# Two of four block sums of the feed-forward weights formed by accumulating DMAs, with the signs of two blocks changed

## Chip, cores and metric

The kernel runs on one core of a Trainium2 chip. The metric is the device time of one execution in microseconds. A core has five engines with a queue each: PE (matrix products), DVE and POOL (elementwise), ACT (elementwise with functions), SP (here it only starts DMAs), and 16 DMA engines, which all queues share.

## The reference

One encoder layer in float32: 512 tokens of width 2048, a mixer of two attentions, then a gated feed-forward network of width 5632. The change touches only the two products that lead from the normed tokens h2 to the feed-forward width:

```python
h2 = rms_norm(x, norm2_w[l]) * (1.0 + sc2) + sh2
ff = (jax.nn.silu(h2 @ w_ffn_gate[l]) * (h2 @ w_ffn_up[l])) @ w_ffn_down[l]
x = x + g2 * ff
```

## The kernel before

**Precision.** PE multiplies a reduced float32 type here. Each float32 tile is split into a high part (a copy on ACT, line 118) and a low part (the rest, a subtraction on DVE, line 119), and each product is made of three matmuls: high by high, high by low, low by high (lines 126 to 128).

**Seven products instead of eight.** Gate and up are computed as 2x2 block products by a scheme of Strassen's kind (Winograd's form): seven block products of sums of blocks instead of eight of blocks. A group (`group7`, line 816) makes 512 columns of gate or of up for all 512 tokens. It adds up over four steps of 512 rows of the weight. 11 groups of columns, gate and up, less the first of gate, which is made with eight products while the tokens' sums are still being formed, give 21 groups and 84 steps.

**One step.** `wforms` (line 767) loads a piece of 512 rows and 512 columns with two DMAs of 512 KB: four blocks b11, b12 (upper rows) and b21, b22 (lower rows), each 128 partitions x 512 numbers. DVE forms four sums: t1 = b12 - b11 and t2 = b22 - t1, the two halves of tile `ta`; t3 = b22 - b12 and t4 = t2 - b21, the two halves of `tb`. Then four tiles are split into high and low: b11 (half a tile), b21 with b22, `ta` and `tb`. Which product uses which half stands in `HALVES[0]`, and PE takes the products in the order of `ORDER`: 1, 2, 3, 5, 6, 7, 4. A product is 12 matmuls of 128x128 by 128x256, so a step has 84.

**Tokens' side.** `xforms` (line 788) forms the same kind of sums of the token blocks a11 to a22 on DVE and POOL, once for each of the four steps, ahead of all groups. Its tiles `sa` and `sb` use the buffers of `ta` and `tb`.

**Group ends.** The seven products stand in seven of the eight banks (`BANK`). After the fourth step ACT copies product 1 and DVE forms the four output blocks (lines 833 to 840) from the banks; the next group writes the same banks. After each up group the two results are multiplied (line 911) and stored (line 912, 1 MB).

**Buffers and order.** Loads into `raw` have 5 buffers, `ta` 2, `tb` 1, the split tiles `whi` and `wlo` 5 each, of which a step uses four, so that the split of one step's tile waits for PE to leave the tile five before it. All plain loads are issued from SP in order. A planner in the tile framework sets the order of instructions in each queue from its own estimates, and so may put work of the next step ahead of the rest of this one; waits on semaphores are put in by the framework.

```python
    ORDER = (1, 2, 3, 5, 6, 7, 4)
    HALVES = ((1,), (2, 3), (5, 6), (7, 4)), ((1,), (2, 4), (5, 6), (7, 3))
    BANK = {1: "mm", 2: "mm", 3: "mm", 5: "mm", 6: "S", 7: "S", 4: "Y"}
```

Of the kernel before, what the change touches and what calls it, by code (L numbers as in the profile page):

```python
# [15 lines left out]
ALU = mybir.AluOpType  # L16
AX = mybir.AxisListType

P = 128
# [65 lines left out]
def encoder_block(ctx: ExitStack, tc, xp, c, w_ada, b_ada, norm1_w, w_in, q_norm_w, k_norm_w, tb,  # L85
                  w_oa, w_ob, w_out, norm2_w, w_gate, w_up, w_down, final_w, rope, wmask, out):
    nc = tc.nc
    V, S, G = nc.vector, nc.scalar, nc.gpsimd
# [11 lines left out]
    def wtile(tag, at=None):  # L100
        at = wbufs["at"] if at is None else at
        return wp.tile([P, 1024 + wbufs["pad"]], F32R, tag=tag, name=tag, bufs=wbufs["w"])[:, at:at + 1024]
    dram = ctx.enter_context(tc.tile_pool(name="dram", bufs=1, space=bass.MemoryType.DRAM))

    def bank(tag):
        return ps.tile([P, 512], F32, tag=tag, name=tag, bufs={"mm": 4, "S": 2, "T": 1, "Y": 1}[tag])
# [10 lines left out]
    def split(hi, lo, src, eng=V):  # L117
        S.activation(hi, src, AF.Copy)  # L118
        eng.tensor_sub(lo, src, hi)  # L119

    def pair(pool, tag, width, bufs):
        return (pool.tile([P, width], F32R, tag=tag + "h", name=tag + "h", bufs=bufs),
                pool.tile([P, width], F32R, tag=tag + "l", name=tag + "l", bufs=bufs))

    def mm3(o, lh, ll, rh, rl, start, stop, **kw):
        nc.tensor.matmul(o, lh, rh, start=start, stop=False, **kw)  # L126
        nc.tensor.matmul(o, lh, rl, start=False, stop=False, **kw)  # L127
        nc.tensor.matmul(o, ll, rh, start=False, stop=stop, **kw)  # L128

    def unit(w, k0, nk, c0, ncol):  # L130
        raw = wp.tile([P, 1024], F32, tag="raw", name="raw", bufs=wbufs["raw"])
        r3 = raw[:, :nk * ncol].rearrange("p (k n) -> p k n", k=nk)
        nc.sync.dma_start(r3, w[k0 * P:(k0 + nk) * P, c0:c0 + ncol].rearrange("(k p) n -> p k n", p=P))
        return raw[:, :nk * ncol], r3
# [96 lines left out]
    t1 = const.tile([P, KT], F32, name="t1")  # L231
# [269 lines left out]
    q = pair(p_a, "q", 4 * T, 1)  # L501
# [56 lines left out]
    q = pair(p_a, "q", 4 * T, 1)  # L558
# [119 lines left out]
    for j in range(0, KT, 2):  # L678
        form1([w_ob], j * P, 2, yT_b, [[bank("mm"), bank("mm")]],
              gated(sg_b[j:], lambda e, g, b: merge(j + e, g, b)))  # L680
        if j >= KT - 6 and len(pre) < 2:
            raw = p_pre.tile([P, 1024], F32, name="praw", tag="praw")
            k0 = 2 * len(pre)
            nc.sync.dma_start(raw.rearrange("p (k n) -> p k n", k=2),
                              w_out[k0 * P:(k0 + 2) * P, :512].rearrange("(k p) n -> p k n", p=P))
            hl = pair(p_pre, f"p{k0}", 1024, 1)
# [62 lines left out]
    HALVES = ((1,), (2, 3), (5, 6), (7, 4)), ((1,), (2, 4), (5, 6), (7, 3))  # L749
# [5 lines left out]
    def half(t, n=2):  # L755
        return t.rearrange("p (a q n) -> p a q n", q=2, n=256) if n == 2 else t.rearrange("p (q n) -> p q n", q=2)

    def split7(parts, tiles, kinds):

        d = {}  # L760
        for (src, views), (hi, lo), rs in zip(parts, tiles, kinds):
            split(hi, lo, src)
            for r, v in zip(rs, views):
                d[r] = (v(hi), v(lo))
        return d

    def wforms(w, k0, c0):
        rt = []
        for a in range(2):
            raw, r3 = unit(w, k0 + 2 * a, 2, c0, 512)  # L770
            rt.append((raw, r3[:, :, :256], r3[:, :, 256:]))
        (_, b11, b12), (r1, b21, b22) = rt
        ta = wp.tile([P, 1024], F32, tag="ta", name="ta", bufs=2)
        tb = wp.tile([P, 1024], F32, tag="tb", name="tb", bufs=1)
        t1, t2_ = (half(ta)[:, a] for a in range(2))
        t3, t4 = (half(tb)[:, a] for a in range(2))
        V.tensor_sub(t1, b12, b11)
        V.tensor_sub(t2_, b22, t1)
        V.tensor_sub(t3, b22, b12)
        V.tensor_sub(t4, t2_, b21)  # L780
        hl = [[wtile(t) for t in ("whi", "wlo")] for _ in range(4)]
        col = lambda e: lambda t: t.rearrange("p (q n) -> p q n", q=2)[:, :, e * 256:(e + 1) * 256]
        blk = lambda e: lambda t: half(t)[:, e]
        g0 = [t[:, :512].rearrange("p (q n) -> p q n", q=2) for t in hl[0]]
        return split7(((b11, (lambda t: t,)), (r1, (col(0), col(1))), (ta, (blk(0), blk(1))), (tb, (blk(0), blk(1)))),
                      [g0] + hl[1:], HALVES[0])

    def xforms(pool, e, o, full=False):

        sa = wp.tile([P, 1024], F32, tag="ta", name="sa", bufs=2)  # L790
        sb = wp.tile([P, 1024], F32, tag="tb", name="sb", bufs=1)
        a11, a21 = e[:, :512], e[:, 512:]
        a12, a22 = o[:, :512], o[:, 512:]
        V.tensor_add(sa[:, :512], a21, a22)
        V.tensor_sub(sa[:, 512:], sa[:, :512], a11)
        G.tensor_sub(sb[:, :512], a11, a21)
        G.tensor_sub(sb[:, 512:], a12, sa[:, 512:])
        tl = [[pool.tile([P, 512 if n == 0 else 1024], F32R, tag=f"x{n}{t}", name=f"x{n}{t}") for t in "hl"]
              for n in range(4)]
        blk = lambda n: lambda t: t[:, n * 512:(n + 1) * 512].rearrange("p (q n) -> p q n", q=2)  # L800
        d = {}
        if full:
            h21 = [wtile(t, 0)[:, :512] for t in ("whi", "wlo")]
            split(*tl[0], a11)
            split(*h21, a21)
            split(*tl[1], o)
            d["21"] = tuple(blk(0)(t) for t in h21)
            for n, rs in ((0, (1,)), (1, (2, 4))):
                for j, r in enumerate(rs):
                    d[r] = tuple(blk(j)(t) for t in tl[n])  # L810
            d.update(split7(((sa, (blk(0), blk(1))), (sb, (blk(0), blk(1)))), tl[2:], HALVES[1][2:]))
            return d
        return split7(((a11, (blk(0),)), (o, (blk(0), blk(1))), (sa, (blk(0), blk(1))), (sb, (blk(0), blk(1)))),
                      tl, HALVES[1])

    def group7(wsrc, xs, order, dst):

        bk = {r: bank(BANK[r]) for r in ORDER}
        for n, s in enumerate(order):
            w = wsrc(s)  # L820
            for r in ORDER:
                (wh, wl), (xh, xl) = w[r], xs[s][r]
                for q in range(2):
                    for c in range(2):
                        o = bk[r][:, c * 256:(c + 1) * 256]
                        cs = slice(c * P, (c + 1) * P)
                        first, last = n == 0 and q == 0 and c == 0, n == len(order) - 1 and q == 1
                        mm3(o, wh[:, q, cs], wl[:, q, cs], xh[:, q], xl[:, q], first, last, skip_group_check=True)
        p = {r: b.rearrange("p (c n) -> p c n", c=2) for r, b in bk.items()}
        (d11, d12), (d21, d22) = dst  # L830
        with tc.high_priority():
            p1 = io.tile([P, 512], F32, tag="io", name="p1").rearrange("p (c n) -> p c n", c=2)
            S.activation(p1, p[1], AF.Copy)
            V.tensor_add(d11, p[2], p1)
            V.tensor_add(d21, p[6], p1)
            V.tensor_add(d12, p[5], d21)
            V.tensor_add(d12, p[3], d12)
            V.tensor_add(d21, p[7], d21)
            V.tensor_add(d22, p[5], d21)
            V.tensor_sub(d21, d21, p[4])  # L840


    wbufs["at"] = 16
# [4 lines left out]
    def raw_tile(name):  # L848
        return wp.tile([P, 1024], F32, tag="raw", name=name, bufs=wbufs["raw"])
# [46 lines left out]
    for n in range(FU):  # L896
        cs = []
        for w in (w_gate, w_up):
            c, v = c_tile()
            cs.append(c)  # L900
            if n == 0 and w is w_gate:
                for f in range(4):
                    S.activation(v[:, f // 2, :, f % 2], banks[f].rearrange("p (t n) -> p t n", t=2), AF.Silu)
                continue
            dst = (v[:, 0, 0], v[:, 1, 0]), (v[:, 0, 1], v[:, 1, 1])
            group7(lambda s: wforms(w, 4 * s, n * 512), hx, range(SU), dst)
            if w is w_gate:
                S.activation(c, c, AF.Silu)
        for a in range(2):
            sl = slice(a * 1024, (a + 1) * 1024)  # L910
            V.tensor_mul(cs[1][:, sl], cs[1][:, sl], cs[0][:, sl])
        (nc.sync if n < FU - 1 else nc.scalar).dma_start(ff_d[n], cs[1])
# [66 lines left out]
    for cc in range(4):  # L979
        hi, lo = pair(p_l, f"w{cc}", 4 * 512, 1)  # L980
        for k in range(0, 4, 2):
            raw, _ = unit(w_down, f0 + k, 2, cc * 512, 512)
# [52 lines left out]
```

## Time and profile before

| what | value |
|---|---|
| median of 3 runs | 2708.28 us (2704.64 to 2709.36) |
| profiled execution | 2707.57 us, span 2705.8 us |
| PE busy | 2602.3 us (96%) |
| DVE busy | 1782.6 us (66%) |
| ACT busy | 968.3 us (36%) |
| POOL busy | 132.9 us (5%) |
| mean granted TensorE clock | 0.986 |

The span runs from the first to the last instruction; 1.8 us of the execution lie outside it. A row of a group reads: line, engine, operation, written tile `<-` read tiles, shapes, count, busy us in all, mean ns of one, and the idle time just before with what ended it. A row of waits reads: waiting engine, its tile and line, `<-`, the releasing engine, tile and line, then us in total, times, and the longest. Instructions that only start a DMA do not count as busy, so SP does not show in the table. `SPq` and `POOLq` are the issuing queues.

### The profile page before, as it was taken

What the parts mean: (1) busy time and instruction counts of PE and PEld (TensorE: products, weight loads), DVE (VectorE), ACT (ScalarE), POOL (GpSimd) and SP (SyncE); (2) the same over time, 40 slices, a digit from 0 to 9 for tenths busy, and PEclk for the clock granted to TensorE, in tenths of its full rate; (3) what the DMA queues carried; (4) which work ended last, traced back from release to release, by engine and by line L of the source; (5) the groups of instructions that cost most, each with busy time, mean ns of one, the idle gap of its engine ahead of it and who ended that gap; (6) DMA issues with size and microseconds to landing.
All of it is one profiled execution on the core that took longest, in us unless ns stands there. A gap on an engine that the chain in (4) does not pass through costs nothing.

```text
span 2705.8 us, 38742 instructions
## 1 busy us (share of the span) xinstructions
PE 2602.3 (96%) x15385; PEld 2286.1 (84%) x15385; DVE 1782.6 (66%) x2556; ACT 968.3 (36%) x1323; POOL 132.9 (5%) x90
## 2 busy tenths in 40 slices
PE   6999898999999998999889999999999999999997
PEld 5788686878888887877789999999999988888886
DVE  7994747356656566665668888888888864343227
ACT  6233344123323233322544444444444432132122
POOL 0001331300000000000010000000000000000000
PEclk9999999999999999999989999999999999999999
DMA  9873233565554677496333433333333455243332
GB/s 307 279 248 117 75 114 105 186 189 161 173 165 150 210 257 233 148 327 212 120 112 120 137 129 124 109 128 125 125 126 125 135 190 182 94 155 125 102 109 86
DMA packets 277157, 427.17 MB, mean 158 GB/s; under 512 B 17008, under 2 KB 140256, under 8 KB 274416
## 3 DMA queue, kind: packets, MB, share of 16 engines
q1 hardware_dynamic: 276640, 423.59, 47.9%
q8 instruction: 121, 1.98, 0.3%
q10 hardware_dynamic: 336, 1.11, 0.1%
q14 instruction: 60, 0.49, 0.1%
HBM read 392.11 MB, written 32.52 MB: 157 GB/s over the span
## 4 chain that ended last, share of the span: by engine, by line
PE 70%; DMA 6%; DVE 4%; ACT 1%; issue 1%; SPq 0%; POOL 0%; DVEq 0%; ACTq 0%; POOLq 0%
PE mm L128 15%; PE mm L127 15%; PE mm L126 15%; PE S L127 5%; PE S L126 5%; PE S L128 5%; DMA raw<-in_w_ada 4%; PE Y L126 2%; PE Y L127 2%; PE Y L128 2%; DVE acc L261 1%; PE T L126 1%; PE T L128 1%; PE T L127 1%; DVE wlo L119 1%
## 5 line engine op out<-in xcount | busy, mean ns | idle before, releaser
L118 ACT ACTIVATE whi<-raw 128x1024 fp32r<-128x1024 f32 (+1 forms) x465 | 453.9, 978 | 988.7 <-PE mm L127 282.1
L119 DVE TENSOR_TENSOR wlo<-raw,whi 128x1024 fp32r<-128x1024 f32 (+1 forms) x433 | 483.1, 1118 | 376.2 <-ACT whi L118 375.6
L261 DVE SCALAR_TENSOR_TENSOR acc<-raw,cact,acc 128x512 f32<-128x512 f32 (+1 forms) x368 | 275.9, 757 | 165.7 <-DMA raw<-in_w_ada 160.5
L119 DVE TENSOR_TENSOR wlo<-ta,whi 128x1024 fp32r<-128x1024 f32 x84 | 102.7, 1223 | 71.5 <-ACT whi L118 71.4
L118 ACT ACTIVATE whi<-ta 128x1024 fp32r<-128x1024 f32 x84 | 89.4, 1065 | 132.1 <-PE mm L127 132.1
L118 ACT ACTIVATE whi<-tb 128x1024 fp32r<-128x1024 f32 x84 | 89.6, 1067 | 123.9 <-PE S L127 123.9
L128 PE MATMUL mm<-x1h,wlo 128*128 128x256 f32 x400 | 110.4, 276 | 0.0
L126 PE MATMUL mm<-x1h,whi 128*128 128x256 f32 x400 | 110.4, 276 | 0.0
L127 PE MATMUL mm<-x1l,whi 128*128 128x256 f32 x400 | 110.4, 276 | 0.0
L119 DVE TENSOR_TENSOR wlo<-tb,whi 128x1024 fp32r<-128x1024 f32 x84 | 102.5, 1221 | 6.3 <-ACT whi L118 3.1
L126 PE MATMUL mm<-x0h,whi 128*128 128x256 f32 x368 | 102.7, 280 | 3.3 <-ACT whi L118 3.3
L128 PE MATMUL mm<-x0h,wlo 128*128 128x256 f32 x368 | 103.1, 280 | 0.8 <-DVE wlo L119 0.8
L127 PE MATMUL mm<-x0l,whi 128*128 128x256 f32 x368 | 102.8, 279 | 0.0
L119 POOL TENSOR_TENSOR wlo<-raw,whi 128x1024 fp32r<-128x1024 f32 x32 | 77.7, 2431 | 407.0 <-ACT whi L118 376.0
L128 PE MATMUL Y<-x1h,wlo 128*128 128x256 f32 x336 | 92.7, 276 | 0.0
L126 PE MATMUL mm<-x3h,whi 128*128 128x256 f32 x336 | 92.7, 276 | 0.0
L127 PE MATMUL mm<-x3l,whi 128*128 128x256 f32 x336 | 92.7, 276 | 0.0
L128 PE MATMUL mm<-x3h,wlo 128*128 128x256 f32 x336 | 92.7, 276 | 0.0
L126 PE MATMUL mm<-x2h,whi 128*128 128x256 f32 x336 | 92.7, 276 | 0.0
L127 PE MATMUL mm<-x2l,whi 128*128 128x256 f32 x336 | 92.7, 276 | 0.0
L128 PE MATMUL mm<-x2h,wlo 128*128 128x256 f32 x336 | 92.7, 276 | 0.0
L126 PE MATMUL S<-x2h,whi 128*128 128x256 f32 x336 | 92.7, 276 | 0.0
(1793 smaller groups left out, 7883.6 us busy)
## 6 DMA issues: line engine op xcount, KB each, us to landing
raw<-in_w_in SPq DMA_DIRECT2D x133, 512.0 KB
raw<-in_w_ada SPq DMA_DIRECT2D x256, 256.0 KB
raw<-in_w_gate SPq DMA_DIRECT2D x88, 512.0 KB
raw<-in_w_up SPq DMA_DIRECT2D x88, 512.0 KB
raw<-in_w_down SPq DMA_DIRECT2D x88, 512.0 KB
raw<-in_w_ada SPq DMA_DIRECT2D x64, 512.0 KB
raw<-in_w_out SPq DMA_DIRECT2D x38, 512.0 KB
ffr<-ffd SPq DMA_DIRECT2D x22, 512.0 KB
```

The lines of the kernel that those rows point to most:

```text
L118: S.activation(hi, src, AF.Copy)
L119: eng.tensor_sub(lo, src, hi)
L126: nc.tensor.matmul(o, lh, rh, start=start, stop=False, **kw)
L127: nc.tensor.matmul(o, lh, rl, start=False, stop=False, **kw)
L128: nc.tensor.matmul(o, ll, rh, start=False, stop=stop, **kw)
L261: V.scalar_tensor_tensor(acc, part, cact[:, k:k + 1], acc, op0=ALU.mult, op1=ALU.add)
```

## The change

b11 is now loaded alone by a DMA of 256 KB into a `raw` tile, b21 with b22 by one of 512 KB as before. b11 is loaded a second time into one half of `ta`, and b22 into the other half, each by a DMA of 256 KB from SP. Then two accumulating DMAs of 256 KB issued from POOL add b12, read from DRAM, to both halves. So `ta` now holds t1 = b11 + b12 and t3 = b12 + b22 without work of DVE, and DVE forms t2 = t1 + b22 and t4 = t2 + b21 in `tb`. b12 no longer gets a tile of its own. The order of products stays; the halves of the tiles now belong to products 5 and 7 (`ta`) and 6 and 4 (`tb`).

Only sums are formed this way, so the signs of blocks b12 and b21 in the scheme are turned against before, and to make up for it those of a12 and a22 in the tokens' sums and some in the output sums.

```diff
     def wforms(w, k0, c0):
-        rt = []
-        for a in range(2):
-            raw, r3 = unit(w, k0 + 2 * a, 2, c0, 512)
-            rt.append((raw, r3[:, :, :256], r3[:, :, 256:]))
-        (_, b11, b12), (r1, b21, b22) = rt
+        blk_of = lambda a, e: w[(k0 + 2 * a) * P:(k0 + 2 * a + 2) * P,
+                                c0 + 256 * e:c0 + 256 * (e + 1)].rearrange("(q p) n -> p q n", p=P)
+        b11 = raw_tile("b11")[:, :512]
+        nc.sync.dma_start(half(b11, 1), blk_of(0, 0))
+        r1, r3 = unit(w, k0 + 2, 2, c0, 512)
+        b21, b22 = r3[:, :, :256], r3[:, :, 256:]
         ta = wp.tile([P, 1024], F32, tag="ta", name="ta", bufs=2)
         tb = wp.tile([P, 1024], F32, tag="tb", name="tb", bufs=1)
-        t1, t2_ = (half(ta)[:, a] for a in range(2))
-        t3, t4 = (half(tb)[:, a] for a in range(2))
-        V.tensor_sub(t1, b12, b11)
-        V.tensor_sub(t2_, b22, t1)
-        V.tensor_sub(t3, b22, b12)
-        V.tensor_sub(t4, t2_, b21)
+        t1, t3 = (half(ta)[:, a] for a in range(2))
+        t2_, t4 = (half(tb)[:, a] for a in range(2))
+        for t, a, e in ((t1, 0, 0), (t3, 1, 1)):
+            nc.sync.dma_start(t, blk_of(a, e))
+        for t in (t1, t3):
+            nc.gpsimd.dma_start(t, blk_of(0, 1), accum_op=ALU.add)
+        V.tensor_add(t2_, t1, b22)
+        V.tensor_add(t4, t2_, b21)
...
-        g0 = [t[:, :512].rearrange("p (q n) -> p q n", q=2) for t in hl[0]]
-        return split7(((b11, (lambda t: t,)), (r1, (col(0), col(1))), (ta, (blk(0), blk(1))), (tb, (blk(0), blk(1)))),
-                      [g0] + hl[1:], HALVES[0])
+        g0 = [t[:, :512] for t in hl[0]]
+        return split7(((b11, (lambda t: half(t, 1),)), (r1, (col(0), col(1))), (ta, (blk(0), blk(1))), (tb, (blk(0), blk(1)))),
+                      [g0] + hl[1:], ((1,), (2, 3), (5, 7), (6, 4)))
...
-        V.tensor_add(sa[:, :512], a21, a22)
+        V.tensor_sub(sa[:, :512], a21, a22)
         V.tensor_sub(sa[:, 512:], sa[:, :512], a11)
         G.tensor_sub(sb[:, :512], a11, a21)
-        G.tensor_sub(sb[:, 512:], a12, sa[:, 512:])
+        G.tensor_add(sb[:, 512:], a12, sa[:, 512:])
...
-            V.tensor_add(d12, p[5], d21)
+            V.tensor_sub(d12, p[5], d21)
             V.tensor_add(d12, p[3], d12)
             V.tensor_add(d21, p[7], d21)
-            V.tensor_add(d22, p[5], d21)
-            V.tensor_sub(d21, d21, p[4])
+            V.tensor_sub(d22, p[5], d21)
+            V.tensor_add(d21, p[4], d21)
```

## The prediction

> **What bounds the kernel now.** I read the profile from coarse to fine: busy tenths over the span, busy time inside the feed-forward stage, who waits there, then one step of it in order of time. First the slices, each 67.6 us wide.
>
> ```profile
> PE   6999898999999998999889999999999999999997
> DVE  7994747356656566665668888888888864343227
> PEclk9999999999999999999989999999999999999999
> DMA  9873233565554677496333433333333455243332
> ```
>
> TensorE is full nearly everywhere. The changed function runs where VectorE stands at 8 (slices 22 to 32). Busy time in four stretches there (columns: stretch, its length, busy us of PE, its weight loads, DVE, ACT, POOL, then clock, share of the 16 DMA engines, GB/s):
>
> ```profile
> 1400.00:1600.00 200.00, 200.00 (x1767) 200.00 (x1767) 164.93 (x203) 89.77 (x96) 0.00 (x0) 1.00 0.37 119
> 1600.00:1800.00 200.00, 200.00 (x1768) 200.00 (x1767) 172.56 (x215) 88.00 (x92) 0.00 (x0) 1.00 0.39 127
> 1800.00:2000.00 200.00, 200.00 (x1767) 200.00 (x1766) 170.61 (x210) 86.30 (x91) 0.00 (x0) 1.00 0.39 127
> 2000.00:2190.00 190.00, 190.00 (x1679) 190.00 (x1678) 160.08 (x197) 83.98 (x88) 0.00 (x0) 1.00 0.38 123
> ```
>
> A busy PE alone could hide short gaps, since its records overlap. The view of waits from 1400 to 2190 us settles it: its whole list of waiters holds ACT and DVE only.
>
> ```profile
> ACT whi L118 <- PE mm L127: 186.1, 165, 4.4
> ACT whi L118 <- PE Y L127: 133.8, 81, 1.7
> ACT whi L118 <- PE S L127: 122.2, 72, 1.7
> DVE wlo L119 <- ACT whi L118: 111.2, 106, 4.3
> ACT whi L118 <- PE Y L128: 1.9, 1, 1.9
> DVE ta L778 <- DMA raw<-in_w_up: 1.4, 3, 0.8
> ACT whi L118 <- ACT whi L118: 0.2, 1, 0.2
> ```
>
> PE never waits; ACT waits for PE to give back the split tiles, DVE waits for ACT. So this stage ends when the matmuls end, at 1.00 granted clock, and DVE at 668.2 of 790 us (85%) is not the bound. One step (one call of the weight function and its 84 matmuls) is read off ACT's order:
>
> ```profile
> 1801.55 1.06 ACT L118 ACTIVATE whi<-ta 128x1024 fp32r<-128x1024 f32 x1 [1.60 <-PE mm L127]
> ...
> 1807.04 0.64 ACT L118 ACTIVATE whi<-raw 128x512 fp32r<-128x512 f32 x1 [1.66 <-PE Y L127]
> ...
> 1816.56 0.64 ACT L118 ACTIVATE whi<-raw 128x512 fp32r<-128x512 f32 x1 [1.65 <-PE Y L127]
> ```
>
> A split into the slot that the last product Y leaves starts at 1807.04 and again at 1816.56: a step is 9.52 us, a product 1.36 us (a seventh). 84 steps make 800 us.
>
> **What the change removes.** Lines 777 and 779:
>
> ```profile
> L777 DVE TENSOR_TENSOR ta<-raw x84: 676/691/694, 1389.4 to 2175.9; 128x512 f32<-128x512 f32 x84
> ```
>
> ```profile
> L779 DVE TENSOR_TENSOR tb<-raw x84: 679/691/695, 1391.1 to 2187.5; 128x512 f32<-128x512 f32 x84
> ```
>
> 2 x 84 x 0.691 = 116 us of DVE. They stand under a full PE, so they give 0 us. The two other subtractions become additions of the same shape: 0. The signs in the x forms and in the output sums change operations, not shapes or engines: 0.
>
> **What it adds, on the DMA engines.** A step issued two 512 KB loads from SP; now SP issues one of 512 KB and three of 256 KB, and POOL two accumulating ones of 256 KB. Rows are 1 KB where they were 2 KB. The price of a packet comes from two stretches, this stage (1400 to 2200) and one with mostly 1 KB rows (600 to 900). Columns: packets, MB, share of 16 engines.
>
> ```profile
> q1 hardware_dynamic: 46587, 98.01, 37.7%
> ```
>
> ```profile
> q1 hardware_dynamic: 45523, 49.24, 52.0%
> ```
>
> 0.377 x 16 x 800 us / 46587 = 103.6 ns for about 2 KB; 0.520 x 16 x 300 / 45523 = 54.8 ns for about 1 KB. A step has 9.52 x 16 = 152.3 us of engine time. Plain loads: 256 x 103.6 + 768 x 54.8 ns = 68.6 us. The rest of the stage (98.01 MB less 161 loads of 0.524 = 13.6 MB, 14% of the 37.7%) takes 8.0 us a step. For 512 accumulating packets no row exists. Low end: the plain 54.8 ns. High end, an estimate: four times that, 219 ns. I take 103.6 ns, the row of the 2 KB packet, because an accumulating packet must also read 2 KB (1 KB from DRAM, 1 KB of the tile). Sum 68.6 + 8.0 + 53.0 = 129.6 of 152.3 us: 85%, from 38%. It fits; it would cease to fit at (152.3 - 76.6) / 512 = 148 ns.
>
> The Trainium skill (Collectives: The Full Stack, section "The bandwidth ceiling: the fold count and why AG ≠ RS ≠ AR") says that an adding transfer runs at half the rate because it has to read two sources. By it a packet would be 2 x 54.8 = 109.6 ns and the load 87%, the same verdict; no run here shows it yet.
>
> **What it adds, in time from buffer to buffer.** Now tile ta (two buffers) is loaded, not computed: SP waits until the tile of two steps earlier is split, loads b11 and b22 into the halves, POOL waits for that and adds b12 to both, then DVE and ACT may read. These rows of DVE give the release and the two places where the result is wanted:
>
> ```profile
> 1802.65 1.22 DVE L119 TENSOR_TENSOR wlo<-ta,whi 128x1024 fp32r<-128x1024 f32 x1 [1.44 <-ACT whi L118]
> 1803.90 0.69 DVE L777 TENSOR_TENSOR ta<-raw 128x512 f32<-128x512 f32 x1
> ```
>
> ```profile
> 1816.20 0.69 DVE L779 TENSOR_TENSOR tb<-raw 128x512 f32<-128x512 f32 x1
> 1816.81 0.69 DVE L780 TENSOR_TENSOR tb<-ta,raw 128x512 f32<-128x512 f32 x1
> ```
>
> Released at 1803.87. The sum t2 for that tile would stand about where L779 stands two steps on, at 1816.20: 12.3 us later. The split of the tile itself falls two steps after 1801.55, at 1820.59: 16.7 us later. So up to 12.3 us nobody notices; up to 16.7 us DVE's queue stands behind t2; beyond that every two steps grow by the excess. What the chain takes comes from two loads of 512 KB:
>
> ```profile
> 1808.60 0.37 SPq L133 DMA_DIRECT2D raw<-in_w_gate  x1
> ```
>
> ```profile
> 1810.70 0.37 SPq L133 DMA_DIRECT2D raw<-in_w_gate  x1
> ```
>
> ```profile
> 1809.00:1809.50 0.50, 0.50 (x6) 0.50 (x6) 0.05 (x1) 0.41 (x1) 0.00 (x0) 1.00 0.00 0
> 1809.50:1810.00 0.50, 0.50 (x7) 0.50 (x6) 0.50 (x1) 0.00 (x0) 0.00 (x0) 1.00 0.48 78
> ...
> 1813.00:1814.00 1.00, 1.00 (x11) 1.00 (x10) 0.97 (x2) 0.16 (x1) 0.00 (x0) 1.00 0.65 242
> 1814.00:1815.00 1.00, 1.00 (x11) 1.00 (x11) 0.87 (x3) 0.91 (x1) 0.00 (x0) 1.00 0.01 4
> ```
>
> The engines are idle until past 1809.50, so bytes move some 1.15 us after the issue at 1808.60; the second load is done about 3 us after its issue. A 256 KB load is 1.15 + 256 x 54.8 / 16 ns = 2.0 us, the second 0.9 us more. For POOL's part in an accumulation (it must issue it, perhaps work on it) there is no row. Low end 0; high end one POOL operation over a 128x1024 tile:
>
> ```profile
> L119 POOL TENSOR_TENSOR wlo<-raw,whi 128x1024 fp32r<-128x1024 f32 x32 | 77.7, 2431 | 407.0 <-ACT whi L118 376.0 <-PE mm L128 17.7 <-PE S L128 13.3
> ```
>
> I take the high end, 2.4, to be safe; then 1.15 to the first byte and 256 x 103.6 / 16 ns = 1.7 us: 5.3 us for one. The first half is ready at 2.0 + 5.3 = 7.3 us, the second, if both run strictly one after the other, at 12.6. With POOL at 0, plain packets and both at once it is 4.9. If the next step's b11 and r1 (2.5 us of engines) get between, 15.1. All below 16.7, and the first half below 12.3: 0 us.
>
> **What moves.** The last pair of blocks changes from {5,6} {7,4} to {5,7} {6,4}: tb is wanted one product earlier (1.36 us), and its slot comes free one product later. Split of tb now starts 6 products into the step before (8.2 us), takes about 2.3 us (as ta: 1801.55 to 1803.87) and is needed after 9.52 + 4 x 1.36 = 15.0 us: 4.5 us spare, 0 us. SP issues 4 DMAs a step at 0.37 us, 1.5 of 9.52 us; the stores of c stand in the same queue. POOL ran nothing in this stage. If the cover goes (PE no longer full), all this DMA waiting shows at once.
>
> **Sum:** 0 us against the profiled execution's 2707.57 us (span 2705.8). The median of the runs shown is 2708.28, 0.7 above. I forecast 2707.5, with an own range of 2702 to 2713.
>
> **Rivals, all but the last slower.**
>
> (1) Late at group ends: 2739 us. Seven banks are emptied by DVE between the steps of two groups.
>
> ```profile
> 1864.16 0.64 ACT L118 ACTIVATE whi<-raw 128x512 fp32r<-128x512 f32 x1 [1.65 <-PE Y L127]
> ```
>
> ```profile
> 1867.09 0.68 DVE L839 TENSOR_TENSOR c<-mm,c 128x512 f32<-128x512 f32 x1
> ```
>
> The new group starts at 1864.16 and wants bank 5 three products later, 1868.24; L839 gives it back at 1867.77. Spare: 0.5 us. If t2 waits for both halves (12.6 us) and a 1 MB store of c (2 x 1.66 us of engines) gets between, it comes at 15.9, 3.6 us after its place; DVE's evacuations queue behind it, and PE loses 3.1 us at each of 10 stores: 31 us. Against it: DVE has 1.4 us a step more room. A stall can also cost clock:
>
> ```profile
> 1380.00:1382.00 2.00, 0.49 (x2) 0.49 (x3) 2.00 (x3) 2.00 (x3) 0.88 (x1) 0.80 0.00 0
> 1382.00:1384.00 2.00, 1.59 (x8) 1.29 (x7) 2.00 (x2) 2.00 (x4) 1.26 (x1) 0.50 0.00 0
> ```
>
> (2) The round trip is the bound: 2775 us. Each us beyond 16.7 costs half a us per step, 42 us in all. If POOL took 4 us per accumulation, 15.1 + 2 x 1.6 = 18.3: 1.6 x 42 = 67 us. For it: no row prices POOL's part. It decides from 3.2 us per accumulation on.
>
> The Trainium skill (SBUF — State Buffer, section "Who interferes with whom") warns that DMAs issued from POOL starve while VectorE holds the port pair both share, and advises the other queues. It exempts two-input operations, which all those of this stage are; no trace here shows either.
>
> (3) The DMA engines are full: 2752 us at three times the plain packet: (76.6 + 512 x 0.1644) / 16 = 10.05 us a step, 0.53 x 84 = 44 us; at four times 11.8 us a step, 2899. Decides from 148 ns on. For it: 1 KB rows and a load of 85% before any queueing.
>
> (4) Faster, 2700: another order in the queues at the stage's two ends, where PE does idle. Nothing in the body can give.
>
> **Chances.** Forecast 0.46, (1) 0.17, (2) 0.17, (3) 0.14, (4) 0.06. This kernel's runs spread by 0.17%, so I call 0.2% (5.4 us) no change: same 0.46, slower 0.48, faster 0.06. The range 2702 to 2800 holds the forecast, (1), most of (2) and the lower half of (3).
>
> **What will show it.** Right: no PE line among the stage's waits, steps of 9.52 us, DVE lower by 1.4 us a step, DMA share near 0.85. Rival 1: PE waiting for DVE once per group, DVE waiting for a DMA into ta. Rival 2: ACT or DVE waiting for ta's DMA at every step with engines below full. Rival 3: DMA share at 1. I am wrong if PE has gaps inside a group.

## The result, and the profile after

The changed kernel takes 2824.76 us in the median of four runs (2823.7 to 2827.16), against 2708.82 us of the kernel before beside it: a ratio of 1.0429, 95% interval 1.041 to 1.0447. The profiled execution took 2824.1 us with a span of 2822.3, 116.5 us more than before. The first split of a `ta` starts at 1401.92 us (1401.76 before), and the last multiplication of gate by up at 2327.08 instead of 2210.39 (before, then after). So the whole loss, 116.7 us, arises between the two, in the changed stage. Beside the experiments below, several kernels, the one before among them, have single runs near 2740 us, about 30 us above their others; why was not examined.

```profile
2210.39 2.35 DVE L911 TENSOR_TENSOR c<-c 128x1024 f32<-128x1024 f32 x2
```

```profile
2327.08 2.35 DVE L914 TENSOR_TENSOR c<-c 128x1024 f32<-128x1024 f32 x2
```

The four stretches of that stage again, same columns (length, busy us of PE, weight loads, DVE, ACT, POOL, clock, DMA share, GB/s):

```profile
1400.00:1600.00 200.00, 186.41 (x1582) 185.31 (x1581) 121.42 (x142) 77.34 (x86) 43.77 (x36) 0.97 0.74 178
1600.00:1800.00 200.00, 184.80 (x1535) 183.56 (x1533) 121.36 (x143) 71.29 (x81) 43.83 (x36) 0.94 0.74 177
1800.00:2000.00 200.00, 185.06 (x1544) 183.87 (x1545) 127.41 (x151) 70.97 (x79) 44.04 (x37) 0.97 0.76 184
2000.00:2190.00 190.00, 175.25 (x1469) 173.90 (x1468) 117.21 (x138) 66.80 (x75) 42.40 (x35) 0.96 0.75 182
```

PE now has gaps: 731.5 of 790 us busy, 58.5 us idle. It also runs slower while it is busy: 6130 matmuls at the 113.2 ns of before (790 us / 6981) would be 693.7 us, so 37.8 us more went to slower matmuls. Together 96 of 790 us. The granted clock explains most of the 37.8: its shortfall (0.03, 0.06, 0.03 and 0.04) times the four stretches is an estimated 32 us. The rest stays open, because PE also has slow stretches at full clock. In the following one, 30 us hold 257 matmuls, where 113.2 ns each would give 265:

```profile
1850.00:1880.00 30.00, 30.00 (x257) 30.00 (x257) 17.86 (x21) 12.32 (x14) 7.30 (x6) 1.00 0.77 188
```

DVE is emptier than ever and the DMA engines are at three quarters.

The waits of the whole stage (1400 to 2300 us), longest first:

```profile
POOL ta L781 <- issue: 619.0, 140, 7.9
DVE wlo L119 <- ACT whi L118: 278.5, 87, 5.9
ACT whi L118 <- DMA ta<-in_w_gate: 239.8, 36, 9.0
ACT whi L118 <- DMA ta<-in_w_up: 152.9, 26, 7.7
PEld mm L126 <- issue: 73.0, 26, 5.1
PE mm L126 <- DVE c L840: 64.7, 19, 4.9
```

Read from below: PE waits for DVE's evacuation L840, 19 times, once in nearly every one of the 21 groups (53.3 of the 58.3 us that it waits from 1400 to 2190), and the weight loads (PEld) stand idle for about as long; ACT waits 62 times for the DMAs into `ta`; and POOL, which issues those, stands 140 times in a wait that no semaphore ends ("issue"). All accumulating DMAs of the run, as a line of the program (duration is what POOL spends on one, landing counts from its issue):

```profile
L781 POOL DMA_DIRECT2D ta<-in_w_up x88: 1203/1213/1317, 1383.6 to 2308.5; - x88
L781 POOL DMA_DIRECT2D ta<-in_w_gate x80: 1204/1213/1224, 1431.6 to 2263.4; - x80
...
DMA to landing us min/median/max: 4.2/4.7/8.8
```

168 of them from 1383.6 to 2308.5 us: one every 5.54 us. Two per step make 11.1 us, where PE needs 9.52. POOL's queue in order of time:

```profile
1825.44 1.22 POOL L781 DMA_DIRECT2D ta<-in_w_gate  x1 [3.55 <-issue]
1831.34 1.21 POOL L781 DMA_DIRECT2D ta<-in_w_up  x1 [4.68 <-issue]
1836.12 1.22 POOL L781 DMA_DIRECT2D ta<-in_w_up  x1 [3.57 <-issue]
1841.21 1.21 POOL L781 DMA_DIRECT2D ta<-in_w_up  x1 [3.87 <-issue]
```

Each starts 4.8 to 5.9 us after the one before, about when that one has landed. The program does not ask for this: in the list of POOL's instructions the second accumulation of a tile waits for its own plain load (DMAHW) alone, the first also for DVE and for the accumulations (DMASW) of the tile two back. None waits for the accumulation just before it.

```
101 L781 DMA ta_12598<-in_w_up 128x2x256 [waits DMASW5_49,DMAHW0_49,DMASW4_49,DVE_49]
102 L781 DMA ta_12598<-in_w_up 128x2x256 [waits DMAHW1_49]
103 L781 DMA ta_12710<-in_w_up 128x2x256 [waits DMASW7_49,DMAHW4_49,DMASW6_49,DVE_49]
104 L781 DMA ta_12710<-in_w_up 128x2x256 [waits DMAHW5_49]
```

What a late accumulation does to PE is seen at a group's end. First ACT:

```profile
1840.99 1.06 ACT L118 ACTIVATE whi<-ta 128x1024 fp32r<-128x1024 f32 x1 [5.91 <-DMA ta<-in_w_up]
```

Then DVE:

```profile
1842.09 1.23 DVE L119 TENSOR_TENSOR wlo<-ta,whi 128x1024 fp32r<-128x1024 f32 x1 [3.05 <-ACT whi L118]
1843.23 0.68 DVE L838 TENSOR_TENSOR c<-S,p 128x512 f32<-128x512 f32 x1
1843.95 0.69 DVE L839 TENSOR_TENSOR c<-mm,c 128x512 f32<-128x512 f32 x1
1844.67 0.69 DVE L840 TENSOR_TENSOR c<-mm,c 128x512 f32<-128x512 f32 x1
```

Then PE:

```profile
1845.51 0.55 PE L126 MATMUL mm<-x3h,whi 128*128 128x256 f32 x1 [3.79 <-DVE c L840]
```

ACT's split of `ta` waits for the DMA, DVE's low part waits for ACT, and the evacuations of the group just finished stand behind it in DVE's queue, so PE does not get back the bank that its third product needs (line 840 reads it last). The same moment in stretches of 2 us, with the clock:

```profile
1842.00:1844.00 2.00, 0.00 (x0) 0.00 (x0) 1.88 (x3) 2.00 (x4) 0.43 (x1) 1.00 0.36 48
1844.00:1846.00 2.00, 0.49 (x2) 0.52 (x3) 1.97 (x4) 0.47 (x1) 0.03 (x1) 0.87 1.02 192
1846.00:1848.00 2.00, 2.00 (x12) 2.00 (x10) 2.00 (x3) 0.00 (x0) 1.19 (x1) 0.50 0.51 158
1848.00:1850.00 2.00, 2.00 (x15) 2.00 (x15) 2.00 (x4) 1.07 (x1) 0.00 (x0) 0.78 0.91 128
```

After a gap of 3.8 us PE goes on at half the clock, which is back at 1.00 in the stretch from 1850 us on.

The software queue of the new DMAs, same stretch of 900 us (packets, MB, share of 16 engines):

```profile
q0 software_dynamic: 44316, 42.72, 33.2%
```

0.332 x 16 x 900 us / 44316 = 107.9 ns a packet. An accumulation (0.262 MB) has 272 packets.

### The profile page after: what moved, and what is told of

It is laid out like the page before. It is cut to its first block, busy times and chain, and to the rows that moved or that the text cites. A ratio compares the mean times of both kernels' runs of the same rounds, so it can differ in the third digit from the quotient of the medians.

```text
span 2822.3 us, 39236 instructions
## 1 busy us (share of the span) xinstructions
PE 2648.6 (94%) x15385; PEld 2324.7 (82%) x15385; DVE 1673.2 (59%) x2388; ACT 950.3 (34%) x1323; POOL 336.9 (12%) x258
## 4 chain that ended last, share of the span: by engine, by line
PE 43%; DMA 16%; issue 10%; DVE 10%; ACT 2%; POOL 1%; SPq 0%; DVEq 0%; ACTq 0%; POOLq 0%
PE mm L126 10%; PE mm L128 10%; PE mm L127 10%; DMA ta<-in_w_gate 5%; DMA raw<-in_w_ada 4%; DMA ta<-in_w_up 4%; DVE wlo L119 4%; PE S L127 3%; PE S L126 3%; PE S L128 3%; DVE acc L261 1%; PE Y L126 1%; PE Y L127 1%; ACT whi L118 1%; PE Y L128 1%
## 5 line engine op out<-in xcount | busy, mean ns | idle before, releaser
L118 ACT ACTIVATE whi<-raw 128x1024 fp32r<-128x1024 f32 (+1 forms) x381 | 399.6, 1051 | 816.2 <-PE mm L127 246.3
L119 DVE TENSOR_TENSOR wlo<-raw,whi 128x1024 fp32r<-128x1024 f32 (+1 forms) x349 | 426.0, 1221 | 327.9 <-ACT whi L118 326.9
L126 PE MATMUL mm<-x3h,whi 128*128 128x256 f32 x336 | 102.2, 304 | 64.7 <-DVE c L840 64.7
L781 POOL DMA_DIRECT2D ta<-in_w_up x88 | 107.2, 1218 | 369.1 <-issue 318.4
L781 POOL DMA_DIRECT2D ta<-in_w_gate x80 | 97.4, 1217 | 352.5 <-issue 313.4
L126 PEld LDWEIGHTS mm<-x3h,whi 128*128 128x128 f32 x336 | 69.6, 207 | 67.9 <-issue 67.9
L126 PE MATMUL mm<-x2h,whi 128*128 128x256 f32 x336 | 100.5, 299 | 4.6 <-DVE c L842 3.6
L128 PE MATMUL mm<-x2h,wlo 128*128 128x256 f32 x336 | 99.2, 295 | 2.4 <-DVE wlo L119 2.3
L128 PE MATMUL mm<-x3h,wlo 128*128 128x256 f32 x336 | 100.3, 298 | 0.0
L127 PE MATMUL mm<-x3l,whi 128*128 128x256 f32 x336 | 100.2, 298 | 0.0
```

The source lines that it names most:

```text
L781: nc.gpsimd.dma_start(t, blk_of(0, 1), accum_op=ALU.add)
```

## Experiments

My theory: the accumulating DMAs run one at a time, and their queue is too slow for the step. First rival: the round trip through the two buffers of `ta` is too long. Second: the DMA engines are too full. Times are medians; each ratio is to the kernel before, run beside it on the same chip, with its 95% interval. It is estimated from the single runs and is not the quotient of the medians.

**A third buffer of `ta`** (one of `raw` given up for it).

```diff
-    wbufs.update(raw=5, w=5, pad=64)
+    wbufs.update(raw=4, w=5, pad=64)
-        ta = wp.tile([P, 1024], F32, tag="ta", name="ta", bufs=2)
+        ta = wp.tile([P, 1024], F32, tag="ta", name="ta", bufs=3)
```

> The changed kernel with three buffers of ta (and four of raw to make room). Theory S (the accumulating DMAs of POOL run one at a time, 168 of them at about 5.5 us, 11 us a step where PE needs 9.52): the rate of the queue is not touched, 2800 to 2835 us, whole list of accumulating DMAs still 5.3 to 5.6 us apart on average. Rival L (the round trip through two buffers of ta is too long, 18 us where 16.7 are free): a third buffer gives 9.5 us more, so 2705 to 2720 us.

Measured 2804.85 us, ratio 1.0309 (1.0204 to 1.0414).

```profile
L781 POOL DMA_DIRECT2D ta<-in_w_up x88: 1203/1213/1319, 1389.7 to 2284.4; - x88
```

168 in 894.7 us, one every 5.36 us. A third buffer takes 20 us off, by what was not worked out; the rate hardly moves. The round trip is not the bound.

**Twice the descriptor store.** The kernel sets 1024 bytes of each SBUF partition aside for the descriptors that POOL writes. The run doubles them; the room came from the padding of the split tiles.

```diff
-    wbufs.update(raw=5, w=5, pad=64)
+    wbufs.update(raw=5, w=5, pad=40)
-    nc = bacc.Bacc("TRN2", target_bir_lowering=False, num_devices=1, dynamic_dma_scratch_size=1024)
+    nc = bacc.Bacc("TRN2", target_bir_lowering=False, num_devices=1, dynamic_dma_scratch_size=2048)
```

> The changed kernel with 2048 bytes per partition set aside for the descriptors of POOL's DMAs instead of 1024 (the split tiles' padding is cut from 64 to 40 numbers to make room). Theory S with the descriptor store as its cause: two accumulating DMAs fit, the second of a tile starts 1.2 to 2 us after the first instead of 4.7, the step goes back to 9.52 us and the time to 2705 to 2720 us. S with another cause (one accumulation at a time in the DMA engines or in POOL's program): still 4.6 to 4.8 us apart, 2815 to 2835 us. Rival D (DMA engines too full, share 0.75): nothing gained, 2815 us or more.

Measured 2760.97 us, ratio 1.0153 (1.0073 to 1.0234): between the two forecasts. The mechanism is as the first theory has it. POOL's queue:

```profile
1804.01 2.45 POOL L781 DMA_DIRECT2D ta<-in_w_up  x2 [6.17 <-DVE wlo L119]
1813.48 2.46 POOL L781 DMA_DIRECT2D ta<-in_w_up  x2 [7.02 <-DVE wlo L119]
```

Both accumulations of a tile go out back to back, and afterwards POOL waits for tiles, not for itself. No PE line is left among the stage's waits. But PE is slower though full and at full clock:

```profile
1600.00:1800.00 200.00, 200.00 (x1694) 200.00 (x1693) 137.69 (x162) 82.41 (x87) 49.11 (x40) 1.00 0.83 202
```

1694 matmuls in 200 us, 118.1 ns each instead of 113.2. That points at the padding.

**The padding alone**, store as it was.

```diff
-    wbufs.update(raw=5, w=5, pad=64)
+    wbufs.update(raw=5, w=5, pad=40)
```

> The changed kernel with the padding of 40 alone, descriptor store as it was: every theory expects 2820 to 2830 us; another time would mean that the padding counts in the run with the larger store.

A single run took 2839.81 us, 15 us above the changed kernel. One time proves little, but the trace shows the slower matmuls without the larger store: 170 in these 20 us with PE full (first row), against 179 in a full stretch of the changed kernel (second row). All 53 stretches of 10 us that are full at a clock of 1.00 have 86 to 88 matmuls (a matmul on an edge counts twice), where 44 of 50 in the changed kernel have 90 or 91. So the padding does count, and my expectation that it would not was wrong.

```profile
1812.00:1832.00 20.00, 20.00 (x170) 20.00 (x170) 12.45 (x15) 6.86 (x8) 4.64 (x4) 1.00 0.86 241
```

```profile
1600.00:1620.00 20.00, 20.00 (x179) 20.00 (x178) 10.42 (x13) 6.00 (x8) 3.97 (x4) 1.00 0.79 184
```

**The larger store with the padding of 64**, room taken from the copies of product 1.

```diff
-    io = tc.alloc_tile_pool(name="io2", bufs=3, side="right", reuse_waits="tile")
+    io = tc.alloc_tile_pool(name="io2", bufs=2, side="right", reuse_waits="tile")
-    nc = bacc.Bacc("TRN2", target_bir_lowering=False, num_devices=1, dynamic_dma_scratch_size=1024)
+    nc = bacc.Bacc("TRN2", target_bir_lowering=False, num_devices=1, dynamic_dma_scratch_size=2048)
```

> The changed kernel with 2048 bytes of descriptor store, the split tiles' padding at 64 as it was, and room made by two buffers instead of three for the copies of product 1 (io). With the padding of 40 the matmuls went at 118.1 ns (1693 in 200 us) instead of 113.2. If the store is the whole cause: 1767 matmuls in 200 us, no PE line among the waits, 2705 to 2720 us. If something of the accumulations stays on the path: above 2725 us.

Measured 2713.46 us, ratio 1.0007 (0.9958 to 1.0056). The stage and its two DMA queues:

```profile
1600.00:1800.00 200.00, 200.00 (x1767) 200.00 (x1766) 146.30 (x174) 88.35 (x92) 51.48 (x42) 1.00 0.85 208
```

```profile
q1 hardware_dynamic: 91601, 120.28, 46.5%
q0 software_dynamic: 45388, 43.75, 38.2%
```

PE is full at its old rate, and the DMA engines carry the whole change at 0.85. This acquits their load: they were less busy (0.75) in the slow kernel.

**Four accumulations of half the size**, store as it was.

```diff
-        for t in (t1, t3):
-            nc.gpsimd.dma_start(t, blk_of(0, 1), accum_op=ALU.add)
+        for q in range(2):
+            for t in (t1, t3):
+                nc.gpsimd.dma_start(t[:, q], w[(k0 + q) * P:(k0 + q + 1) * P, c0 + 256:c0 + 512], accum_op=ALU.add)
```

> The changed kernel, store of 1024 bytes as it was, each accumulating DMA cut in two of 128 KB (four per step, half the descriptors each). Theory S with the descriptor store as its cause: two or three fit at once, issues 0.6 to 2 us apart in bursts, time 2705 to 2740 us. If each accumulation has a fixed cost of its own that they pay one after another: four of 3.5 us or more, 14 us a step, above 3000 us.

Measured 2711.7 us, ratio 0.9968 (0.9928 to 1.0008).

```profile
1804.60 2.67 POOL L782 DMA_DIRECT2D ta<-in_w_up  x3 [7.36 <-DMA ta<-in_w_up]
1809.30 0.86 POOL L782 DMA_DIRECT2D ta<-in_w_up  x1 [2.03 <-issue]
```

Three halves go out at once and the fourth waits: the store holds three halves but not four, so one whole accumulation but not two. Counted in packets of the software queue (an estimate: 47816 for 43.54 MB are 144 a half), three halves are 432 and fit, while four halves (576) or two whole accumulations (544) do not. Same bytes, twice the DMAs, and the loss is gone; a fixed cost that accumulations pay one after another is excluded.

**Plain copies from POOL** in place of the accumulations, so the sums with b12 are left out.

```diff
-            nc.gpsimd.dma_start(t, blk_of(0, 1), accum_op=ALU.add)
+            nc.gpsimd.dma_start(t, blk_of(0, 1))
```

> The changed kernel with POOL's two DMAs per step as plain copies of b12 over the halves (the sums with b12 are left out: b12 alone stands in their place). If accumulating is what makes them slow: landing falls from 4.7 to about 3 us, two take 6 to 7 us of a step, time 2705 to 2720 us. If it is the queue of POOL and not the accumulation: landing stays at 4.2 to 4.7 us and the time at 2800 to 2830 us.

Measured 2728.87 us, ratio 1.0055 (1.0007 to 1.0104), with runs from 2711.85 to 2745.25 (four of eight above 2737); the kernel before ranged from 2705.8 to 2740.17 beside it (two of thirteen above 2737). The profiled execution, 2711.85 us, has 1767 matmuls in 200 us and no PE wait in the stage.

```profile
1801.48 1.45 POOL L781 DMA_DIRECT2D ta<-in_w_up  x2 [9.27 <-DVE wlo L119]
```

```profile
q0 software_dynamic: 13188, 43.22, 16.7%
```

Two plain copies go out back to back in the old store, at 0.72 us of POOL each instead of 1.21. Per MB they cost 0.167 x 16 x 800 / 43.22 = 49 us of engine time; the accumulations of the run with the larger store cost 0.382 x 16 x 800 / 43.75 = 112. The run fits neither forecast whole: the time is that of the first (in its profiled execution), the landing, median 4.3 us, that of the second. The number in flight decides, not the single landing: with the larger store and the padding of 64 an accumulation landed after 6.6 us in the median, later than the 4.7 of the changed kernel, and nothing was lost. Nor does this run separate the accumulating from the store, since a plain copy goes in fewer packets: 13188 for 43.22 MB are 80 a copy, against 272 for an accumulation. So two copies would fit where two accumulations do not.

**One accumulation per step**, t3 on DVE.

```diff
+        r0, q3 = unit(w, k0, 2, c0, 512)
+        b11, b12 = q3[:, :, :256], q3[:, :, 256:]
...
+        nc.sync.dma_start(t1, blk_of(0, 0))
+        nc.gpsimd.dma_start(t1, blk_of(0, 1), accum_op=ALU.add)
+        V.tensor_add(t3, b22, b12)
```

> Half of the change: t1 by one accumulating DMA per step, t3 on DVE (b11 with b12 loaded as before). Theory S: one of 5.5 us in a step of 9.52 us: 2705 to 2720 us. A theory in which the two buffers' round trip counts: load 2 us, one accumulation 5 us, also 2705 to 2720 us. Above 2725 us would speak against both.

Measured 2713.09 us, ratio 1.0004 (0.9958 to 1.0051). One fits into 9.52 us; it landed after 5.9 to 6.1 us in the median.

**The signs and pairs without the DMAs.**

```diff
+        V.tensor_add(t1, b11, b12)
+        V.tensor_add(t3, b22, b12)
         V.tensor_add(t2_, t1, b22)
         V.tensor_add(t4, t2_, b21)
```

> The change without its DMAs: new signs, new pairs of halves, all four sums on DVE from two loads of 512 KB as before. All theories: within 0.2% of the kernel before, steps of 9.52 us.

Measured 2713.92 us, ratio 1.0031 (0.9993 to 1.0068), profiled span 2706.9 us, 1767 matmuls in 200 us. The ratio is a little above the 0.2% that I expected, with 1 inside its interval; the new signs and pairs cost nothing that can be seen here.

**A padding of 32** with the larger store, to see what it was about the padding of 40.

```diff
-    wbufs.update(raw=5, w=5, pad=64)
+    wbufs.update(raw=5, w=5, pad=32)
-    nc = bacc.Bacc("TRN2", target_bir_lowering=False, num_devices=1, dynamic_dma_scratch_size=1024)
+    nc = bacc.Bacc("TRN2", target_bir_lowering=False, num_devices=1, dynamic_dma_scratch_size=2048)
```

> As the run with the larger descriptor store and the padding cut from 64 to 40, but cut to 32 (a split tile is 4224 bytes per partition, a multiple of 64, instead of 4256; with 64 it is 4352, a multiple too). If the slower matmuls (118.1 ns) came from tiles that begin off a multiple of 64 bytes: 1767 matmuls in 200 us, 2705 to 2720 us. If from a shorter padding as such: 1690 or fewer in 200 us, 2755 us or more.

Measured 2722.4 us, ratio 1.0007 (0.9961 to 1.0053).

```profile
1600.00:1800.00 200.00, 200.00 (x1768) 200.00 (x1766) 144.53 (x170) 88.25 (x93) 51.52 (x42) 1.00 0.84 209
```

The stage is back at 113.2 ns, while the time is 2.4 us above the range that I expected. A shorter padding as such is not the cause; tiles that begin at multiples of 64 bytes fit the three paddings in this stage.

## Why the prediction was wrong

**Right.** PE bounded the stage, and the DVE work taken off gave nothing: DVE fell from 85% to 62% of the stage (71% with the larger store and the padding of 64, where the step was 9.52 us again) and no run became faster. The signs, the pairs of halves and the plain loads cost nothing that can be seen (runs with DVE sums and with the larger store and the padding of 64). An accumulating packet, taken at 103.6 ns, measured 107.9, twice the 54.8 of a plain one; the Trainium skill (Collectives: The Full Stack, section "The bandwidth ceiling: the fold count and why AG ≠ RS ≠ AR") gave half the rate, and the trace agrees. The load of 85% came out as 0.85 where the step was 9.52 us. That it fits so exactly is luck: by parts, accumulations took 58 us of engine time a step instead of 53 (0.382 x 152.3), and the DMAs from SP 71 instead of 77 (0.465 x 152.3). Rival 3 was rightly the weakest of the slower ones.

**The step that failed** is "What it adds, in time from buffer to buffer". I put one accumulation at 5.3 us, allowed that both halves might run "strictly one after the other", and compared the sum of one tile, 12.6 us, with the 16.7 us its round trip had. I did not compare the queue's rate with the step: two in series are 2 x 5.3 = 10.6 us and a step is 9.52. With that line the same numbers give (10.6 - 9.52) x 84 = 91 us, 2798 us. Measured were 5.54 us each and 116 us (5.54 in that line gives 131; why 116 of them show was not worked out). The whole of 5.3 us was nearly right, in part by luck: POOL's part was 1.21 us instead of 2.4, the time from there to the landing 3.5 instead of 2.85, and some 0.8 us more passed before the next started. The test was the wrong one. The two accumulations of a tile were held up by those of the other tile before them, so a tile whose plain loads were issued at 1822.82 could be split only at 1840.99, 18.2 us later.

```profile
1822.82 0.92 SPq L779 DMA_DIRECT2D ta<-in_w_up  x2
```

**What made them serial** I left open; the two runs with the larger store and full-speed matmuls (padding of 64 and of 32) and the run with four halves show it: the descriptor store of 1024 bytes held one accumulation of this size. The Trainium skill (DMA: Bandwidth & Descriptors, section "SWDGE vs HWDGE vs iDMA") says that descriptors of DMAs issued from GpSimd stand in rings in an area of SBUF; the runs agree in so far as the size of the area set aside decided (2824.76 us with 1024 bytes, 2713.46 with 2048). The same page (section "🔬 Anatomy of one DMA — SWDGE (gpsimd) path") puts a DMA at 2.0 us and its bytes at 436 GB/s, which for 256 KB would be an estimate of 2.6 us and two well within a step; the accumulations landed after 4.7, and the measurement decides.

**Rival 2** came nearest by kind: POOL's DMAs as the bound. Its price (4 us of POOL's time per accumulation, 2775 us) and its cause were wrong. POOL spends 1.21 us on one (1203 to 1317 ns over all 168); the rest is waiting for room. Its sign came nearly as named: ACT waited for the DMAs into `ta` 62 times in 84 steps with the DMA engines at 0.75. A third buffer would have cured rival 2 as I described it, and did not cure the kernel.

**Rival 1** named the place where PE would lose, DVE's evacuations at group ends, and that half clock follows. But it hung this on the stores of c and ten group ends; it happened at 19, with 3.4 us each (64.7 us). It reckoned with the bank of product 5 (0.5 us spare); PE waited for that of product 3, which had 0.9 us at the same group end before (line 837 ends at 1865.98, the product is due at 1866.88). That PE loses there, and not inside a group, is put down to this small slack; no run tests it, and it is not the cause of the late accumulations.

## What to carry to other kernels

When work is handed to a queue, make two tests: the time of one round trip against the buffers, and the time of all its pieces in a step against the step. Ask how many pieces may be in flight; if the store for descriptors holds one, latency turns into rate. Where an engine is full and never waits, taking work off another can at best do nothing, and here smaller pieces (0.9968, 0.9928 to 1.0008) or more room only got that nothing back.

## What the runs showed beside the question

The padding of the split tiles counts for PE: with tiles of 4256 bytes per partition matmuls of 256 columns took 118.1 ns, with 4224 and 4352 bytes 113.2 wherever PE was full throughout the stage, at a granted clock of 1.00 in all three. The cause (tiles that begin at a multiple of 64 bytes or something else) was not tested further. In the stage of the last product, where the tiles begin at another offset, the padding of 32 was slower as well, though 4224 is a multiple of 64: 434 matmuls in 100 us against 443.

```profile
2250.00:2350.00 100.00, 100.00 (x434) 81.20 (x434) 34.27 (x36) 20.51 (x20) 0.00 (x0) 1.00 0.35 115
```

The padding is not all of it. In the run with the third buffer of `ta`, whose padding is 64, PE has slow and fast stretches, all full and at a granted clock of 1.00; here are 258 and 267 matmuls in 30 us. The cause stays open.

```profile
1630.00:1660.00 30.00, 30.00 (x258) 30.00 (x257) 18.80 (x22) 11.26 (x13) 7.30 (x6) 1.00 0.84 219
1930.00:1960.00 30.00, 30.00 (x267) 30.00 (x266) 17.14 (x19) 10.55 (x13) 6.53 (x6) 1.00 0.82 190
```

So a change of memory layout that is made to gain room has to be timed by itself.
